# A decoder layer on one core: the recurrence's links cut into three steps, attention's calls between them in a fixed order, first query projections traced ahead of the inverse table

## The chip, the core and the metric

The kernel runs on one core of one Trainium2 chip. The metric is the device time of an execution in microseconds. TensorE (PE, with its weight loads PEld) multiplies, VectorE (DVE), ScalarE (ACT) and GpSimd (POOL) compute on the results, and SyncE (SP) issues the DMAs of this kernel, in order.

## The reference, cut to what matters

A layer takes x of 512 tokens by 1024 and adds three things to it in turn: half of a SwiGLU network, a mixing part, and half of a second SwiGLU network. The mixing part is the one that the change touches:

```python
proj = h @ w_in[l]
q, k, v, rr, rk, rv, rc = jnp.split(proj, split_idx, axis=-1)
...
att = dilated_attention(qh, kh, vh).transpose(0, 2, 1, 3).reshape(b, s, ATT_WIDTH)
rw = rwkv7_time_mix(rr, rk, rv, rc, ...)
x = x + jnp.concatenate([att, rw], axis=-1) @ w_out[l]
```

Attention has 8 heads of 64 and merges three dilated windows. The recurrence has 8 heads of 64, each with a 64x64 state that every token decays, corrects and adds to:

```python
sa = jnp.einsum('bhij,bhj->bhi', state, a_t)
state = state * w_t[:, :, None, :] + sa[..., None] * b_t[:, :, None, :] + v_t[..., None] * k_t[:, :, None, :]
return state, jnp.einsum('bhij,bhj->bhi', state, r_t)
```

## The kernel before

**Stages.** The first network runs to about 380 us, the mixing part to about 770 us (its output projection the last of it), the second network to the end. Matrices are kept as a high and a low fp32r half, and a product is three matmuls of 512 columns (`mm3`, L72), so one 128-column tile of a projection is 24 matmuls. The halves of a weight tile are made by ScalarE (L68) and by VectorE (L69) or POOL, from a load that SP issues (L64); there are two buffers of each half.

**The recurrence in chunks.** Its 512 tokens are cut into 8 chunks of 64. Inside a chunk the recurrence becomes triangular matrices, whose inverses `invert` (L632) makes on VectorE for all chunks and heads at once, 31 steps of two instructions; it ends with two transposes, ud and td, and with eight copies that make tm and um (L654, L655). `whole` (L661), called for each of four channel tiles, forms the off-diagonal blocks of the inverse table tbd: four products w, copies, four products u, copies.

**The chain.** `chain` (L855) is one link: for a pair of channel tiles and one chunk it multiplies the state into the chunk (cx, L866), multiplies that with the table (cs, L877) and forms the next state and the output (cn, L883). VectorE or ScalarE copies lie between the three. There are 16 links, (gi, c) with gi and c from 0 to 3; gi is a pair of tiles and a half of the sequence, and links of one pair depend on each other. `pre` (L805) loads and prepares a group of four links, `post` (L891) normalizes and gates its output. Both are generators in two parts.

**Attention.** `qkv` (L685) projects queries, keys and values of a channel tile (two heads) and is a generator that stops in the middle of each projection and between them. `attention` (L790) is a pipe of three: each call issues `scores` of a new unit (tile, block of 128 queries, head), `turned` (transposes) of the unit two calls back, and `weighted` of the unit three calls back. For the second head of a pair `weighted` ends with the transposition oT (L772) of what VectorE's rd and o (L768, L770) have made.

**What sets the order.** The framework's scheduler orders each engine's instructions at build time by readiness in its own model, and among ready ones by the order in which they were traced. `tc.high_priority()` puts what is traced in it ahead of older work. `tc.keep_in_program_order(t)` binds an instruction behind the one traced before it on its engine. Each engine then executes its instructions strictly in that order. The trace order of links, attention, projections, `pre` and `post` comes from a list of events with due times, sorted by time and then by a rank:

```python
ev += [(4 * gi + c, 4, lambda gi=gi, c=c: link(gi, c)) for gi in range(4) for c in range(4)]
ev += [(4 * gi + t, 5, lambda gi=gi: next(posts[gi], 0)) for t, gi in
       [(3, gi) for gi in range(4)] + list(zip((3.9, 3.9, 4.8, 4.5), range(4)))]
ev += [(4 * gi + c + t, 6, lambda u=(gi, c, h): attention(u)) for gi, t in enumerate((1.6, 1.0, 0.0, 0.0))
       for c in range(4) for h in range(2)]
for e in sorted(ev, key=lambda e: e[:2]):
    e[2]()
```

**Stores and ticks.** Operands of the chain pass through HBM tensors (ard, bkd, bvd). `put_stores` (L403), called in every projection of the recurrence, issues up to four stores that were collected before the last call, in program order on SP. `tick` (L396) runs work that was put off by so many half projections, as the bonus product (`bonus`, L623).

## Time and profile before

| | |
|---|---|
| Median of 3 runs | 1137.75 us (1137.55 to 1143.27) |
| Profiled execution | 1137.26 us, its span 1135.5 us |
| PE busy | 1100.3 us, 97% of the span, 5512 matmuls |
| DVE, ACT, POOL busy | 492.4, 383.9, 142.2 us |
| PE's granted clock, mean | 0.991 |

The page gives busy time by engine, the span in 40 slices, the chain of work that ended last and the costliest groups of instructions. A busy matmul is counted with its way through the array, so matmuls that follow each other every 0.23 us are shown as 0.39 us long and overlap. A number in square brackets behind an instruction is the idle time of its engine before it, with what ended it.

### The profile page before, as it was taken

Reading aid. Unit: us, or ns where it says so; the run is one execution under the profiler, and the core shown is the slowest. Engines: PE = TensorE matmul, PEld = TensorE weight load, DVE = VectorE, ACT = ScalarE, POOL = GpSimd, SP = SyncE. Lnnn points to the kernel's source line nnn. Section 1 sums busy time; section 2 is a strip of 40 time slices with the busy share of each in tenths; the row PEclk is TensorE's granted clock in tenths of the full one; section 3 lists DMA queues with packets and bytes.
Section 4 is the critical chain, followed back from the end, with each engine's and each line's share of the span. In section 5 each row is a group of like instructions: output and inputs, shape, how many; then the busy total and the mean of one; then the engine's idle time right before and its main releaser. Section 6 shows DMA issues by size and latency. Waiting matters only on the chain.

```text
span 1135.5 us, 13760 instructions
## 1 busy us (share of the span) xinstructions
PE 1100.3 (97%) x5512; PEld 918.6 (81%) x5512; DVE 492.4 (43%) x811; ACT 383.9 (34%) x604; POOL 142.2 (13%) x189
## 2 busy tenths in 40 slices
PE   7999999999999999898899999999999999999998
PEld 6888888888888977676788888789888888888887
DVE  5333333332223545594467568644333333332222
ACT  4332223222222356524344544433322232222120
POOL 3000000000000346303342221112000000000000
PEclk9999999999999999998989999999999999999999
DMA  5322322233224424442422201422223322233321
GB/s 189 111 93 94 104 99 93 93 98 103 96 93 146 164 70 102 121 123 82 130 57 66 84 29 29 141 83 94 93 93 103 101 93 93 96 103 101 126 94 56
DMA packets 53202, 111.88 MB, mean 99 GB/s; under 512 B 20721, under 2 KB 26097, under 8 KB 53138
## 3 DMA queue, kind: packets, MB, share of 16 engines
q1 hardware_dynamic: 53138, 111.00, 30.6%
q8 instruction: 43, 0.70, 0.3%
q14 instruction: 21, 0.17, 0.0%
HBM read 100.50 MB, written 9.44 MB: 97 GB/s over the span
## 4 chain that ended last, share of the span: by engine, by line
PE 48%; DVE 2%; POOL 2%; ACT 1%; issue 1%; POOLq 0%; ACTq 0%
PE gu L76 7%; PE gu L77 7%; PE gu L73 7%; PE accd L76 4%; PE accd L73 4%; PE accd L77 4%; PE in L77 1%; PE in L73 1%; PE in L76 1%; PE aa L840 1%; PE acco L76 1%; PE cn L883 1%; PE acco L77 1%; PE acco L73 1%; PE cx L866 1%; PE po L764 1%
## 5 line engine op out<-in xcount | busy, mean ns | idle before, releaser
L68 ACT CAST hi_gu<-raw_gu 128x1024 fp32r<-128x1024 f32 x88 | 92.8, 1054 | 316.2 <-PE gu L76 303.6
L69 DVE TENSOR_TENSOR lo_gu<-raw_gu,hi_gu 128x1024 fp32r<-128x1024 f32 x84 | 102.9, 1225 | 158.3 <-ACT hi_gu L68 154.3
L76 PE MATMUL accd<-lo_d,hh 128*128 128x512 f32 x288 | 112.3, 390 | 0.0
L77 PE MATMUL accd<-hi_d,hl 128*128 128x512 f32 x288 | 112.1, 389 | 0.0
L73 PE MATMUL accd<-hi_d,hh 128*128 128x512 f32 x288 | 112.0, 390 | 0.0
L69 DVE TENSOR_TENSOR lo_d<-raw_d,hi_d 128x1024 fp32r<-128x1024 f32 x44 | 53.3, 1224 | 127.5 <-ACT hi_d L68 127.1
L68 ACT CAST hi_d<-raw_d 128x1024 fp32r<-128x1024 f32 x44 | 45.6, 1053 | 152.7 <-PE accd L77 133.0
L198 DVE TENSOR_TENSOR sg<-gu,sg 128x512 f32<-128x512 f32 x44 | 30.4, 692 | 143.5 <-PE gu L77 142.1
L76 PE MATMUL gu<-xa0l,hi_gu 128*128 128x512 f32 (+1 forms) x184 | 70.0, 380 | 0.3 <-DVE xa0l L130 0.3
L73 PE MATMUL gu<-xa0h,hi_gu 128*128 128x512 f32 (+1 forms) x184 | 70.2, 381 | 0.1
L73 PE MATMUL gu<-xc0h,hi_gu 128*128 128x512 f32 (+1 forms) x184 | 70.0, 380 | 0.0
L73 PE MATMUL gu<-xa1h,hi_gu 128*128 128x512 f32 (+1 forms) x184 | 70.0, 380 | 0.0
L73 PE MATMUL gu<-xc1h,hi_gu 128*128 128x512 f32 (+1 forms) x184 | 70.0, 380 | 0.0
L76 PE MATMUL gu<-xc0l,hi_gu 128*128 128x512 f32 (+1 forms) x184 | 69.9, 380 | 0.0
L77 PE MATMUL gu<-xa0h,lo_gu 128*128 128x512 f32 (+1 forms) x184 | 69.9, 380 | 0.0
L77 PE MATMUL gu<-xa1h,lo_gu 128*128 128x512 f32 (+1 forms) x184 | 69.9, 380 | 0.0
L76 PE MATMUL gu<-xa1l,hi_gu 128*128 128x512 f32 (+1 forms) x184 | 69.9, 380 | 0.0
L77 PE MATMUL gu<-xc0h,lo_gu 128*128 128x512 f32 (+1 forms) x184 | 69.9, 380 | 0.0
L76 PE MATMUL gu<-xc1l,hi_gu 128*128 128x512 f32 (+1 forms) x184 | 69.9, 380 | 0.0
L77 PE MATMUL gu<-xc1h,lo_gu 128*128 128x512 f32 (+1 forms) x184 | 69.9, 380 | 0.0
L76 PEld LDWEIGHTS accd<-lo_d,hh 128*128 128x128 f32 x288 | 54.1, 188 | 11.6 <-DVE lo_d L69 0.5
L77 PEld LDWEIGHTS accd<-hi_d,hl 128*128 128x128 f32 x288 | 54.1, 188 | 11.3
(349 smaller groups left out, 2250.2 us busy)
## 6 DMA issues: line engine op xcount, KB each, us to landing
raw_gu<-in_ffn_w_gu SPq DMA_DIRECT2D x88, 512.0 KB, 3.4
raw_d<-in_ffn_w_down SPq DMA_DIRECT2D x44, 512.0 KB, 3.4
raw_in<-in_w_in SPq DMA_DIRECT2D x28, 512.0 KB, 3.8
raw_o<-in_w_out SPq DMA_DIRECT2D x8, 512.0 KB, 3.4
x<-in_x SPq DMA_DIRECT2D x4, 512.0 KB, 6.4
xd<-x SPq DMA_DIRECT2D x4, 512.0 KB, 2.6
xr<-ard SPq DMA_DIRECT2D x8, 256.0 KB, 4.5
bk<-bkd SPq DMA_DIRECT2D x4, 512.0 KB, 4.3
```

The source lines that it names most:

```text
L68: A.copy(out=hi, in_=raw)
L69: (lo_eng or V).tensor_tensor(out=lo, in0=raw, in1=hi.bitcast(F32), op=ALU.subtract)
L73: first = T.matmul(ps, lh, rh, start=start, stop=False)
L76: T.matmul(ps, lh, rl, start=False, stop=False)
L77: T.matmul(ps, ll, rh, start=False, stop=stop)
L198: V.tensor_tensor(out=sg, in0=ps[1], in1=sg, op=ALU.mult)
L764: T.matmul(po[:, h, 0:65], pw[:, j * P:(j + 1) * P], va[:, j, h, 0:65], start=(j == 0), stop=(j == qi))
L840: T.matmul(ps[:, c], bk[:, j, c], xr[:, j, c, 2 * h:2 * h + 2], start=True, stop=True)
L866: T.matmul(px[:, j, h], xr[:, j, c, 2 * h:2 * h + 2].rearrange("p a b -> p (a b)"), sv[:, j, h, c, :], start=True, stop=True)
L883: T.matmul(pn[:, j, h], kr[:, j, c, 2 * h:2 * h + 2].rearrange("p a b -> p (a b)"), sv[:, j, h, c, :], start=True, stop=True)
```

## The change

`put_stores` keeps stores back for one more call (`recent`). In `invert` the four copies of tm move from POOL to VectorE. In `whole` the first product w of a tile is bound in program order. `qkv` stops once more, after the query projection. The query projections of tiles 0 and 1 are traced right after `invert`, each followed by a tick, and `whole` after them, without ticks of its own. `chain` becomes a generator in three steps, the first matmul of each bound in program order; it is no longer traced at high priority. The due times of attention, of the projections of tiles 2 and 3 and of `post` are set anew, so that each link's steps are due at 0, 0.3 and 0.6 of its slot and two attention calls at 0.1 and 0.4 from slot 1 on.

```diff
--- before.py
+++ after.py
@@ -398,13 +398,14 @@
         for f in due.pop(turn[0], ()):
             f()
 
-    stores, older = [], []
+    stores, recent, older = [], [], []
 
     def put_stores():
 
         for out_, in_ in older[:4]:
             tc.keep_in_program_order(Q.dma_start(out=out_, in_=in_))
-        older[:] = older[4:] + stores
+        older[:] = older[4:] + recent
+        recent[:] = stores
         stores.clear()
 
     def proj_parts(j, ct):
@@ -651,7 +652,7 @@
         um, tm = (tmp([P, NCT, 4, 32], n) for n in ("um", "tm"))
         for h in range(2):
             for e in range(2):
-                G.tensor_copy(out=tm[quad(h, e)], in_=tv[quad(h, 0), :, :, e])
+                V.tensor_copy(out=tm[quad(h, e)], in_=tv[quad(h, 0), :, :, e])
                 G.tensor_copy(out=um[quad(h, 1 - e)], in_=uv[quad(h, 1), :, :, e])
         return ud.rearrange("p (a b c) t -> p a b c t", a=NCT, b=2), um, tm
 
@@ -668,7 +669,9 @@
         G.memset(w, 0.0)
         ps = pt([P, 4, 32], f"w{ct}")
         for m in range(4):
-            T.matmul(ps[:, m, :], R[ct]['nof'][:, m, :], tm[:, ct, m, :], start=True, stop=True)
+            t = T.matmul(ps[:, m, :], R[ct]['nof'][:, m, :], tm[:, ct, m, :], start=True, stop=True)
+            if m == 0:
+                tc.keep_in_program_order(t)
         for h in range(2):
             for e in range(2):
                 q_ = quad(h, 1 - e)
@@ -686,6 +689,7 @@
         tq = lambda shape, name: gp.tile(shape, F32, tag="tq", bufs=2, name=name)
         at = lambda shape, n, t=F32R: gp.tile(shape, t, tag=f"at{n}", bufs=2, name=f"{n}{ct}")
         acc = yield from proj_parts(0, ct)
+        yield
         sq = tq([P, S], f"sqq{ct}")
         A.activation(out=sq, in_=acc, func=AF.Square)
 
@@ -862,9 +866,11 @@
         jh = [(j, h) for j in range(2) for h in range(2)]
 
         px = pc([P, 2, 2, CH], f"cx{nm}")
-        for j, h in jh:
-            T.matmul(px[:, j, h], xr[:, j, c, 2 * h:2 * h + 2].rearrange("p a b -> p (a b)"), sv[:, j, h, c, :],
-                     start=True, stop=True)
+        for n, (j, h) in enumerate(jh):
+            t = T.matmul(px[:, j, h], xr[:, j, c, 2 * h:2 * h + 2].rearrange("p a b -> p (a b)"), sv[:, j, h, c, :],
+                         start=True, stop=True)
+            if n == 0:
+                tc.keep_in_program_order(t)
         xc = spool.tile([P, 2, 2, CH], F32, tag="cx", bufs=2, name=f"xc{nm}")
         V.tensor_copy(out=xc, in_=px)
         if not last:
@@ -872,16 +878,22 @@
             for h in range(2):
                 V.tensor_tensor(out=sp[half(h)], in0=sv[half(h), :, h, c, :],
                                 in1=pend[cp][half(h), :, cg:cg + 1].broadcast_to([64, 2, CH]), op=ALU.mult)
+        yield
         pa = pc([P, 2, 2, CH], f"cs{nm}")
         for j in range(2):
-            T.matmul(pa[:, j], tbd[:, gi, j, c, :], xc[:, j], start=True, stop=True)
+            t = T.matmul(pa[:, j], tbd[:, gi, j, c, :], xc[:, j], start=True, stop=True)
+            if j == 0:
+                tc.keep_in_program_order(t)
         A.copy(out=sv[half(0), :, 0, c, :], in_=pa[half(0), :, 0])
         V.tensor_copy(out=sv[half(1), :, 1, c, :], in_=pa[half(1), :, 1])
 
+        yield
         pn = ps_y.tile([P, 2, 2, CH], F32, tag="y", name=f"cn{nm}")
-        for j, h in jh:
-            T.matmul(pn[:, j, h], kr[:, j, c, 2 * h:2 * h + 2].rearrange("p a b -> p (a b)"), sv[:, j, h, c, :],
-                     start=True, stop=True)
+        for n, (j, h) in enumerate(jh):
+            t = T.matmul(pn[:, j, h], kr[:, j, c, 2 * h:2 * h + 2].rearrange("p a b -> p (a b)"), sv[:, j, h, c, :],
+                         start=True, stop=True)
+            if n == 0:
+                tc.keep_in_program_order(t)
         if not last:
             for h in range(2):
                 V.tensor_tensor(out=nxt[half(h), :, h], in0=pn[half(h), :, h], in1=sp[half(h)], op=ALU.add)
@@ -937,11 +949,14 @@
     for ct in range(NCT):
         rates(ct)
     inv = invert()
+    parts = [qkv(ct) for ct in range(NCT)]
+    for ct in range(2):
+        next(parts[ct])
+        next(parts[ct])
+        tick()
     for ct in range(NCT):
         whole(ct, *inv)
-        while due:
-            tick()
-    for out_, in_ in older + stores:
+    for out_, in_ in older + recent + stores:
         Q.dma_start(out=out_, in_=in_)
     pstack.close()
     gp = mc.enter_context(tc.tile_pool(name="gp", bufs=1, reuse_waits="tile"))
@@ -966,22 +981,22 @@
         for z in held:
             hilo(mixT[z[0]], *z[1:])
 
-    def link(gi, c):
-        with nullcontext() if gi == 2 else tc.high_priority():
-            chain(gi, c)
-
-
-    parts = [qkv(ct) for ct in range(4)]
-    ev = [(t, 1, lambda ct=ct: next(parts[ct], 0)) for ct, t0, dt in ((0, -1.0, 0.05), (1, -0.5, 0.05), (2, 4.0, 0.6), (3, 7.8, 0.6))
-          for t in (t0 + dt * n for n in range(6))]
+    links = {(gi, c): chain(gi, c) for gi in range(4) for c in range(4)}
+
+
+    ev = [(t, 1, lambda ct=ct: next(parts[ct], 0)) for ct, ts in enumerate((
+          (-1.0, -0.95, -0.9, -0.85, -0.8), (-0.5, -0.45, -0.4, -0.35, -0.3),
+          (2.8, 3.8, 4.8, 5.8, 6.4, 6.8, 7.4), (7.8, 8.4, 8.8, 9.4, 9.8, 10.4, 10.8))) for t in ts]
     ev += [(11.0, 1, mix)]
     ev += [(t, 2 + n, lambda gi=gi: next(pres[gi], 0)) for gi, ts in enumerate(((-2, -2), (2, 2), (5, 6), (9, 9)))
            for n, t in enumerate(ts)]
-    ev += [(4 * gi + c, 4, lambda gi=gi, c=c: link(gi, c)) for gi in range(4) for c in range(4)]
+
+    ev += [(4 * gi + c + t, 4, lambda gi=gi, c=c: next(links[gi, c], 0)) for gi in range(4) for c in range(4)
+           for t in (0, 0.3, 0.6)]
     ev += [(4 * gi + t, 5, lambda gi=gi: next(posts[gi], 0)) for t, gi in
-           [(3, gi) for gi in range(4)] + list(zip((3.9, 3.9, 4.8, 4.5), range(4)))]
-    ev += [(4 * gi + c + t, 6, lambda u=(gi, c, h): attention(u)) for gi, t in enumerate((1.6, 1.0, 0.0, 0.0))
-           for c in range(4) for h in range(2)]
+           [(3.7, gi) for gi in range(4)] + list(zip((4.3, 4.3, 4.8, 4.5), range(4)))]
+    ev += [(t + 0.1 + 0.3 * h, 6, lambda u=(ct, qi, h): attention(u)) for ct, ts in enumerate(
+           ((1, 2, 3, 4), (5, 6, 7, 7.5), (8, 9, 10, 11), (12, 13, 14, 15))) for qi, t in enumerate(ts) for h in range(2)]
     for e in sorted(ev, key=lambda e: e[:2]):
         e[2]()
     step = begin(mixT)
```

## Rows read from the trace of the kernel before

**Rows 1.** busy us (instructions) of PE, PEld, DVE, ACT, POOL; PEclk, DMA, GB/s

```profile
476.00:521.00 45.00, 40.19 (x163) 31.05 (x161) 42.11 (x84) 12.58 (x19) 3.83 (x4) 0.96 0.39 118
521.00:548.00 27.00, 21.76 (x115) 18.21 (x116) 8.07 (x19) 10.49 (x29) 11.03 (x19) 0.87 0.28 88
526.00:532.00 6.00, 5.76 (x19) 4.95 (x20) 1.70 (x3) 1.02 (x3) 3.75 (x8) 0.56 0.13 29
548.00:584.00 36.00, 33.15 (x202) 29.02 (x200) 19.20 (x50) 13.24 (x26) 16.33 (x22) 0.91 0.34 95
584.00:714.00 130.00, 124.20 (x877) 111.44 (x877) 93.41 (x271) 62.89 (x131) 32.82 (x37) 1.00 0.17 52
```

**Rows 2.** timeline of TensorE: start us, us, instruction, idle before and its releaser

```profile
482.77 0.50 PE L77 MATMUL in<-xb0h,lo_in 128*128 128x512 f32 x1 [2.82 <-DVE lo_in L69]
484.02 0.63 PE L73 MATMUL in<-xb0h,hi_in 128*128 128x512 f32 x1
```

**Rows 3.** timeline of TensorE round the inverse table's first product

```profile
520.37 0.39 PE L73 MATMUL in<-xb1h,hi_in 128*128 128x512 f32 x1
520.60 0.39 PE L76 MATMUL in<-xb1l,hi_in 128*128 128x512 f32 x1
526.24 1.91 PE L671 MATMUL w<-tm,nof 128*128 128x32 f32 x8 [5.26 <-POOL tm L654]
```

**Rows 4.** timelines of VectorE, POOL and ScalarE, the same columns

```profile
518.63 2.14 DVE L648 STREAM_TRANSPOSE td<-tu 128x1024 f32<-128x1024 f32 x1
...
525.58 0.61 POOL L654 COPY tm<-td 32x512 f32<-32x512 f32 x1
...
511.10 0.68 ACT L519 ACTIVATE v<-in,dv 128x512 f32<-128x512 f32 x1
```

**Rows 5.** groups on VectorE, 521 to 715: busy us, mean ns | idle before

```profile
L869 DVE COPY xc<-cx 128x256 f32<-128x256 f32 x16 | 6.7, 421 | 6.1 <-PE cx L866 5.6
...
L675 DVE COPY w<-w 32x128 f32<-32x128 f32 x8 | 2.3, 283 | 2.6 <-ACT w L675 2.5
...
L628 DVE TENSOR_TENSOR bv<-bo,v 128x512 f32<-128x512 f32 x1 | 0.7, 692 | 0.4 <-PE bo L626 0.4
```

**Rows 6.** timelines of POOL and VectorE during the inversion

```profile
477.67 1.19 POOL L615 TENSOR_TENSOR rt<-r,pb 128x512 f32<-128x512 f32 x1 [10.45 <-DVE r L520]
...
477.75 1.18 DVE L641 TENSOR_TENSOR pr<-au,tu 128x60 f32<-128x60 f32 x1
478.97 0.23 DVE L643 TENSOR_TENSOR tu<-tu,pr 128x60 f32<-128x60 f32 x1
```

**Rows 7.** TensorE's waits, 521 to 556 and 556 to 584: us, times, longest

```profile
PE in L73 <- ACT kts L704: 1.7, 1, 1.7
...
PE spk L511 <- ACT rbk L507: 1.2, 1, 1.2
```

**Rows 8.** timeline of TensorE at a link late in the chain

```profile
699.88 0.71 PE L877 MATMUL cs<-xc,tbd 128*128 128x128 f32 x4 [0.52 <-DVE xc L869]
```

**Rows 9.** TensorE's waits, 584 to 715

```profile
PE cn L883 <- DVE sv L879: 1.2, 2, 0.6
PE cs L877 <- DVE xc L869: 1.0, 2, 0.5
```

**Rows 10.** timelines of VectorE and TensorE at two of attention's outputs

```profile
596.62 0.15 DVE L768 RECIPROCAL rd<-po 128x2 f32<-128x2 f32 x1
...
598.18 0.29 DVE L770 TENSOR_TENSOR o<-po,rd 128x128 f32<-128x128 f32 x1
...
728.06 0.48 PE L76 MATMUL acco<-lo_o,mx0h 128*128 128x512 f32 x1
...
729.00 0.33 PE L772 MATMUL oT<-ident,o 128*128 128x128 f32 x1
```

**Rows 11.** timeline of TensorE, first output product on the recurrence's last part

```profile
733.18 0.84 PE L73 MATMUL acco<-hi_o,mx1h 128*128 128x512 f32 x3
```

**Rows 12.** timeline of ScalarE at a weight load

```profile
500.19 1.05 ACT L68 CAST hi_in<-raw_in 128x1024 fp32r<-128x1024 f32 x1 [1.75 <-DMA raw_in<-in_w_in]
```

## The prediction

> **What bounds the kernel now.** I read the page's engine table first: TensorE is busy almost all of the span, so whatever moves the end must shorten TensorE's stream, its waits or its slow clock. The change touches the mixing stage alone, and the second view cuts that by stretches [rows 1]. The idle time of a stretch is its length less PE's busy time. From 476 to 521 us it is 4.8 us, but there VectorE is busy 42.1 of 45 us with the triangular inversion, and TensorE waits for weight halves that VectorE makes [rows 2]; the change lightens none of that. After it the idle is 5.2 us (521 to 548), 2.9 (548 to 584) and 5.8 (584 to 714). The granted clock adds to that: 0.56 over the 6 us from 526 means 5.3 us at half speed, so 2.6 us lost; 0.91 over the 36 us from 548 means 6.5, so 3.2 us lost. The ceiling of any gain is 13.9 of idle and 5.8 of clock, 19.7 us. Then I read who waits for whom inside each stretch, and single timelines.
>
> **Part A, the inverse table (521 to 548 us).** TensorE's last projection matmul starts at 520.60; then TensorE stands 5.26 us until the fourth copy of tm has left POOL [rows 3]. VectorE had finished td at 518.63 + 2.14 = 520.77; POOL made tm and um by turns and began its fourth tm at 525.58 [rows 4].
> The headline move, query projections ahead of the table, I cost at nothing. ScalarE reads the last values accumulator of the recurrence at 511.10 [rows 4], so the matmuls from there to 520.6, 0.23 us apart [rows 3], are attention's projections already: the scheduler had put some 41 of them there. The change fixes that place and swaps a key projection for the second query projection, of the same size. The pin on the first table product adds no wait, since it stood behind these in any case. Without such cover 9.5 us would lie bare, but the pin forbids just that.
> The copy is what pays. No row shows a VectorE copy of 32x512 from SBUF. The nearest are copies from PSUM, 0.283 us with 128 elements and 0.421 with 256 [rows 5]: 0.14 for 128 more, so 0.70 with 512. Four cost 1.1 us if size were free and 2.8 by the slope; I take the slope, since both rows bear it. tm is then complete at 523.6, at best at 521.9, and at worst, with the last bonus product (0.69) [rows 5] ahead on VectorE, at 524.3. TensorE is done with projections at 520.8 and with the last bonus product, which now comes first, near 521.3. It waits 2.3 us (0.6 to 3.0) in place of 5.26: 3.0 us gained (2.3 to 4.7). For the clock the neighbour is a wait of 2.82 us, after which matmuls took 0.63 us [rows 2], not the usual 0.39 [rows 3]. 2.3 is shorter, by how much it must be no row says, so I take half of the 2.6 us. If a weight half also gets ahead of tm, most of the gain goes; that is the lower bound. **A: 4.3 us, from 1 to 7.**
> Behind tm's copies on VectorE stands the weight half of the key projection that fills the pauses of the table's products; it comes 2.8 us later, while TensorE runs the first products.
> One observation speaks against the split. A POOL product from 477.67 to 478.86 reads SBUF, and a VectorE product that began in it took 1.18 us, the next of its size 0.23 [rows 6]: the two held each other up. The Trainium skill, "SBUF — State Buffer", section "Who interferes with whom", says that POOL and a VectorE copy in a two-port mode exclude one another for a whole instruction; no row of before shows a copy doing that. By that rule tm's first copy would wait for um's last. um can start at 518.8 and takes about 0.6 us four times, so it ends near 521.3: 0.5 us less gain, inside the bounds. The same skill, "VectorE: DVE Perf Modes", section "Mode 2×_2P", would have such a copy make two elements a cycle; an estimate from its 0.96 GHz is 0.27 us each, and A would be nearer 6. The sum here goes by rows, and by neither.
>
> **Part B, from the table to the first links (548 to 584 us).** Lost now: 2.9 us of idle, namely 1.7 at a projection whose accumulator ScalarE had not yet freed and 1.2 at a transposition waiting for ScalarE's spread [rows 7], and 3.2 us of clock. Here links 0 to 3 lie among projections of tiles 0 and 1. After the change the first link is traced behind all of these, so the stretch becomes dense 512-column matmuls. TensorE now draws some 45 projection matmuls, 10 us, into the table's 27; if A is shorter some 15 of them are left over, 3.5 us, and cover the 1.7. The spread's chain then runs beside a whole projection. Against that, link 0 has no attention between its steps: three waits, each as the 0.52 us of a bare link [rows 8], 1.6 us unless later work floats up. I take 4 of the 6.1. **B: +4, from -1.6 to +6.**
>
> **Part C, links with attention (584 to 714 us).** Of the idle 5.8 us, waits of link steps are 1.2 at cn and 1.0 at cs [rows 9]: 2.2 us is all that filling can return, as links and attention overlap already. An attention call's scores, transposes and weighted products last longer than the 0.52 us they have to cover.
> The added wait hides in the pin. The cs step is held behind the instruction traced before it on TensorE, and every other attention call ends with the transposition oT, which waits for VectorE's rd and o. In the last unit TensorE was free at 728.06 and oT ran at 729.00: 0.94 us [rows 10]. Behind it on TensorE would stand cs and cn, and behind those the next link. Fifteen links have it. Fillers are projection halves up to link 10, and later the next unit's scores and transposes, so I charge 0.1 us a link, 1.5 in all. **C: +0.7, from -12 (nothing fills: 14.1 less 2.2) to +2.2.** Dropping the links' high priority costs nothing as long as trace order puts them first anyway.
>
> **Part D, the tail.** The last link and the last post now follow both last attention calls. The first matmul on that post's result ran at 733.18 [rows 11], 19 us after the last link, and those 19 us have to be filled from what is left; some 3 us of it, the two calls, have gone ahead. Output matmuls that need attention alone can still come forward. **D: -1, from -3 to 0.**
>
> **Stores.** Each goes out one projection later on SP's in-order queue, where weight loads stand behind it. A late load reached an engine visibly once: ScalarE waited 1.75 us for it [rows 12], and TensorE did not. I take 0 (0 to 1.7). Stores that fall behind the table delay the reloads after it, which the dense projections of B cover; bare, a pair of loads costs its landing. Tiles 2 and 3's seven parts and the later posts shift work between links: nothing, while TensorE has other work.
>
> **Sum.** 4.3 + 4 + 0.7 - 1 = 8.0 us off the profiled execution's 1137.26 gives 1129.3. The median of the three runs lies 0.5 higher, 1129.8; I round to 1129.5.
>
> **Rivals.**
> *VectorE sets the table after all.* tm goes behind the bonus product and a weight half, table products start near 525.5, the clock still falls, and the slack that feeds B is missing: A 1, B 1, C and D as above, 1.7 us in all, about 1136. For: VectorE is 94% busy until 521. Against: tm is traced ahead of that half. The same time comes out if the change doesn't do what it says: a pin binds one instruction to the one before, and later work may float past it into the old order. I count both as one.
> *oT paces the links*, the slower one. Its price then includes VectorE's queue: at 596.62 + 0.15 rd was done, and o came at 598.18 [rows 10], 1.4 us after it could. 0.94 + 1.4 less 0.8 of filler is 1.5 a link, 23 us for fifteen. With A, B, D and the 2.2 gained (9.5 us) that is 1137.3 - 9.5 + 23 = 1151. It decides from 0.63 us a link on (no gain), and from 1.04 it is over 0.5% slower. For: o waited behind other VectorE work there. Against: the pin makes o urgent in the order, and projections are at hand for ten links.
> *All of it fits*: A 7, B 6, C 2.2, D 0, 15.2 us, 1122. For: each idle place has a named cause. Against: B needs both waits and the clock.
>
> **Chances.** Forecast 0.45, VectorE (or old order) 0.25, oT 0.18, all of it 0.12. About 0.5% is what a measurement of this kernel tells from no change; the bounds are 1132.1 and 1143.4. The forecast's own spread, A from 1 to 7 and B from -1.6 to 6, has a little on the wrong side, the rivals a little on the right: faster 0.57, same 0.25, slower 0.18. The range leaves out most of the oT case and the end of the best: 1119 to 1143.
>
> **What would show it.** A: the wait before the first w matmul between 0.6 and 3 us and named VectorE's tm; full clock from 526. B: granted clock 1.0 where links 0 to 3 begin, no wait at spk. C: waits at cs for oT or o would be the slower rival; cn and cs without waits, the forecast. D: more idle before 733's counterpart. I am wrong if idle plus lost clock from 521 to 714 does not fall below some 12 us, or if the stretch before 521, held unchanged, moves by over 2 us.

## The result and the profile after

The changed kernel takes 1150.62 us (median; 1148.69 to 1151.61) against 1137.65 for the kernel before: a ratio of 1.0108, 95% interval 1.0074 to 1.0142. It is 1.1% slower, 13.0 us, where 1129.5 had been forecast. The profiled execution took 1151.33 us with a span of 1149.5; its mean granted clock is 0.982, before 0.991. Runs of one kernel differ in their mean granted clock (the kernel before from 0.982 to 0.992), so medians below come with their lowest and highest run where that matters.

The first view gives the same stretches as [rows 1], and two more (the stretch and its length; busy us and instructions of PE, PEld, DVE, ACT, POOL; PEclk; DMA; GB/s):

```profile
476.00:521.00 45.00, 39.46 (x166) 30.59 (x164) 43.35 (x87) 13.41 (x23) 7.71 (x10) 1.00 0.39 117
521.00:548.00 27.00, 23.60 (x118) 19.77 (x119) 11.26 (x25) 13.11 (x32) 7.90 (x17) 0.82 0.34 101
548.00:584.00 36.00, 33.12 (x220) 28.97 (x219) 17.54 (x50) 14.37 (x27) 15.09 (x14) 0.95 0.32 93
584.00:714.00 130.00, 120.01 (x777) 106.67 (x775) 84.42 (x241) 52.48 (x109) 29.43 (x34) 0.93 0.16 49
598.00:621.00 23.00, 19.22 (x114) 17.77 (x113) 16.80 (x45) 8.71 (x19) 6.17 (x7) 0.78 0.12 35
705.00:719.00 14.00, 12.34 (x55) 11.49 (x55) 6.87 (x25) 5.51 (x14) 3.12 (x3) 0.52 0.01 2
```

From 521 to 714 us TensorE idles 3.4 + 2.9 + 10.0 = 16.3 us (13.9 before), and the clock takes 4.9 + 1.8 + 9.1 = 15.8 (before 3.5 + 3.2 = 6.7 if counted so; the prediction's 5.8 leaves out half clock while TensorE stood). The link stretch, at full clock before, has it now at 0.93; the last two rows are where. In the second of them the clock is at the lower of its two levels (1.2 of 2.4 GHz) nearly throughout.

Clock times of the two kernels are no longer comparable, so the second cut goes by events: from the last table product (547.3 before, 542.8 after) to the last projection product, and from there to the first transposition of the next network (757.2 and 771.3). First before, then after:

```profile
547.30:685.70 138.40, 132.05 (x885) 117.60 (x885) 89.81 (x249) 61.07 (x123) 43.76 (x52) 0.98 0.23 69
685.70:757.20 71.50, 67.30 (x404) 57.35 (x403) 47.49 (x114) 32.75 (x67) 12.63 (x16) 1.00 0.29 97
```

```profile
542.80:691.00 148.20, 136.19 (x881) 120.24 (x881) 88.64 (x248) 60.61 (x123) 42.66 (x52) 0.94 0.22 67
691.00:771.30 80.30, 72.59 (x403) 62.33 (x402) 48.26 (x116) 32.48 (x67) 12.15 (x16) 0.91 0.23 83
```

TensorE's instructions are the same in number, within four in each part. The changed kernel arrives 4.5 us earlier, then loses 9.8 us while projections last and 8.8 us after them: 14.1 in all (the spans differ by 14.0). By kind, TensorE's busy time over the whole span grows from 1100.3 to 1109.4 us with the same 5512 matmuls, and its idle time from 35.2 to 40.1: some 9 of the 14 us are products at half clock (the mean clock's fall by 0.009 gives 10), 5 are waiting. In the second part nothing but links, attention and posts is there until the output projection, which starts only behind the last link: 29.0 us without a projection before (685.7 to 714.7), 42.1 after (691.0 to 733.1).

Who TensorE waits for, 543 to 771 (us, times, longest), the counterpart of [rows 7, 9]:

```profile
PE yo L928 <- DVE ysb L923: 3.3, 2, 1.7
PE in L73 <- ACT kts L708: 2.8, 1, 2.8
PE sc L744 <- DVE mx L748: 2.1, 1, 2.1
PE spk L512 <- ACT rbk L508: 1.9, 1, 1.9
PE po L768 <- DVE pw L759: 1.6, 2, 1.4
PE oT L776 <- DVE o L774: 1.4, 3, 0.7
...
PE cs L884 <- DVE xc L875: 0.8, 2, 0.5
```

Of these names yo and gg are transposes and gate products of `post`, aa products of `pre`, kts and spk belong to the keys of `qkv`, and sc, po and oT to attention. The link steps themselves hardly wait: cs 0.8 in all, cx and cn not at all. The waits stand in what lies ahead of them. Two stretches of TensorE's timeline show it (start, duration, instruction, idle before and its releaser). From link 4 to link 5:

```profile
598.95 0.56 PE L768 MATMUL po<-va,pw 128*128 128x65 f32 x4
601.59 0.51 PE L744 MATMUL sc<-kh,qs 128*128 128x512 f32 x1 [2.08 <-DVE mx L748]
...
607.58 0.78 PE L893 MATMUL cn<-sv,kr 128*128 128x64 f32 x6
...
610.75 1.05 PE L496 MATMUL hsq<-cst,sqq 128*128 128x2 f32 x8 [1.04 <-ACT o L934]
...
617.04 3.52 PE L844 MATMUL aa<-xr,bk 128*128 128x128 f32 x16
620.32 0.47 PE L73 MATMUL in<-xb0h,hi_in 128*128 128x512 f32 x1
620.63 1.05 PE L844 MATMUL aa<-xr,bk 128*128 128x128 f32 x8
621.52 1.00 PE L870 MATMUL cx<-sv,xr 128*128 128x64 f32 x8
```

Link 4 is done at 608.36 and link 5's own input is there at 609.06 (VectorE's sv, 608.46 + 0.60), but link 5 begins at 621.52, pinned behind all 32 aa products of the next group. Between 596.3 and 620.3 no projection begins. From link 12 to link 13:

```profile
704.94 1.34 PE L893 MATMUL cn<-sv,kr 128*128 128x64 f32 x8
...
710.83 1.12 PE L928 MATMUL yo<-ident,ysb 128*128 128x128 f32 x4 [1.66 <-DVE ysb L923]
711.74 1.92 PE L940 MATMUL gg<-sg,g 96*128 96x256 f32 x4
713.45 1.81 PE L870 MATMUL cx<-sv,xr 128*128 128x64 f32 x8
```

Link 13 needs nothing from yo and gg, products of the third post, but is pinned behind them; its own input was there at 706.94 (VectorE's sv, 706.33 + 0.61).

### The profile page after: what moved, and what is told of

Same layout as the page of the kernel before. It is cut to its first block, busy times and chain, and to the rows that moved or that the text cites. A ratio compares the mean times of both kernels' runs of the same rounds, so it can differ in the third digit from the quotient of the medians.

```text
span 1149.5 us, 13743 instructions
## 1 busy us (share of the span) xinstructions
PE 1109.4 (97%) x5512; PEld 926.6 (81%) x5512; DVE 494.1 (43%) x815; ACT 383.9 (33%) x604; POOL 138.1 (12%) x185
## 4 chain that ended last, share of the span: by engine, by line
PE 84%; DVE 7%; POOL 3%; ACT 3%; issue 2%; DMA 1%; SPq 0%; POOLq 0%; ACTq 0%; DVEq 0%
PE gu L73 14%; PE gu L76 14%; PE gu L77 14%; PE accd L76 7%; PE accd L73 7%; PE accd L77 7%; PE in L73 3%; PE in L77 3%; PE in L76 2%; PE aa L844 1%; PE cn L893 1%; DVE pr L642 1%; PE acco L77 1%; PE acco L73 1%; PE acco L76 1%
## 5 line engine op out<-in xcount | busy, mean ns | idle before, releaser
L73 PEld LDWEIGHTS accd<-hi_d,hh 128*128 128x128 f32 x288 | 53.9, 188 | 11.5 <-ACT hi_d L68 0.4
```

The lines of the kernel that those rows point to most:

```text
L73: first = T.matmul(ps, lh, rh, start=start, stop=False)
```

## The experiments

Ratios are to the kernel before, with 95% intervals.

### Which half loses?

The first half alone: before with the change's edits to `put_stores`, `invert` and `whole` and its early query projections; links, events and priority stay.

```diff
+        if ct < 2:
+            yield
...
-          for t in (t0 + dt * n for n in range(6))]
+          for t in (t0 + dt * n for n in range(5 if ct < 2 else 6))]
```

> Before with the change's first half alone: tm's copies on VectorE, stores kept back for one more call, the query projections of tiles 0 and 1 traced ahead of the table's products, the pin on the first w. Links, events and priority as before. Theory: the loss of the change sits in the links, and this half is the gain that the trace of after shows at the last u (542.78 us against 547.33, 4.55 us ahead); the links then run as before, so about 1133 us (1130 to 1135). Rival: this half is what upsets the later stages, because projections of tiles 0 and 1 that used to lie among the first links are gone; then 1140 or more.

Measured: 1142.71 us (1130.13 to 1145.08), ratio 1.002 (0.9988 to 1.0051). Its fastest run has a mean clock of 0.995, its slowest 0.979. The profiled one shows where (the granted clock is the third column from the end):

```profile
696.00:718.00 22.00, 20.71 (x94) 19.68 (x95) 11.59 (x39) 7.79 (x19) 3.10 (x3) 0.53 0.01 1
```

So neither expectation holds as it stands. The rival's time came (1140 or more), though not among the first links alone: the gain is there in some runs, and in the profiled one most of it is lost to half clock behind the last projection.

The links' half alone: after with those edits undone.

```diff
-          (-1.0, -0.95, -0.9, -0.85, -0.8), (-0.5, -0.45, -0.4, -0.35, -0.3),
+          (-1.0, -0.95, -0.9, -0.85, -0.8, -0.78, -0.75), (-0.5, -0.45, -0.4, -0.35, -0.3, -0.28, -0.25),
```

> After with the first half taken back: tm on POOL, stores as before, no early query projections, no pin on w; chain in three pinned steps, no high priority and the new due times stay. Theory: this half loses all that after loses behind the last u, 18.7 us (228.5 us from there to the first output tile of the next network against 209.9), so about 1155 us (1151 to 1158). Rival (the first half is to blame): 1137, as before.

Measured: 1155.26 us, 1.0169 (1.0142 to 1.0196). The theory's time came: the links' half loses 17.6 us, and the first half gives back 4.6 of them.

### Does oT pace the links?

```diff
-        ps = pt([P, P], f"oT{ct}{qi}")
-        T.transpose(out=ps, ...)
+        AT['late'] = lambda: outputs(ct, qi, o)   # run behind the next call's scores
```

> After with attention's transposition oT and what follows it issued in the next attention call behind that call's scores, so that no link step stands directly behind an oT that waits for VectorE; pins, due times and the rest stay. The recorded slower rival (oT paces the links, 1.5 us a link): 10 us or more come back, 1140 or less. The theory of pins behind preparations and posts: waits that name oT and its inputs are 1.4 to 2 us in all in after, so 1148 to 1151.

Measured: 1146.90 us, 1.0092 (1.0073 to 1.0110): 3.7 us back, not 10, and more than the other theory's 1148 to 1151 allowed. The recorded slower rival had the right time for the change, 1151, but its mechanism is worth a quarter of what it charged.

### The pins

Without the pins on cx, cs and cn (the edit for cx is shown, the others are like it):

```diff
             t = T.matmul(px[:, j, h], ...)
-            if n == 0:
-                tc.keep_in_program_order(t)
```

> After without the program-order pins on cx, cs and cn; due times, three steps, priority and the first half stay. Theory: the pins lose the time, since they hold each link behind group preparations, posts and ScalarE's and VectorE's work for these, and then TensorE's clock falls in the sparse stretches; without them most of 18.7 us comes back: about 1135 us (1131 to 1140). Rival A, the new due times and the lost high priority do it: 1147 to 1151. The recorded slower rival (oT in front of cs) also expects about 1135 here.

Measured: 1145.62 us, 1.0071 (1.0046 to 1.0095): 5.0 us back, a third of what was expected. The rest stays with what is left of the links' half: the due times, the three steps and the lost high priority, which no run separates.

The edit above alone, the pins on cs and cn kept:

> After without the pin on each link's first step cx alone; the pins on cs and cn stay. Theory: what the pins cost (5.0 us, 1150.6 against 1145.6 without any) is that cx waits behind group preparations and posts, as link 0 behind spk, link 5 behind the aa products and link 13 behind yo and gg: 1146 to 1148. Rival: cs and cn behind attention's and VectorE's work cost it: 1150 to 1151.

Measured: 1143.98 us (1143.08 to 1148.37), 1.0068 (1.0041 to 1.0096). 6.6 us come back, so the pin on cx carries all of the pins' cost; those on cs and cn cost nothing that can be told.

### The hole in the projections

In the changed kernel no half of tile 2's projections is due between 3.8 and 5.8: the hole. The changed kernel with these due times at about those of before:

```diff
-          (2.8, 3.8, 4.8, 5.8, 6.4, 6.8, 7.4),
+          (4.0, 4.6, 4.65, 5.2, 5.8, 6.4, 7.0),
```

> After with the parts of tile 2's projections due at about the times of before (4.0, 4.6, 4.65, 5.2, 5.8, 6.4, 7.0 in place of 2.8, 3.8, 4.8, 5.8, 6.4, 6.8, 7.4); pins stay. In after no projection half is due between 3.8 and 5.8, and from about 598 to 620 us TensorE has only small matmuls; the clock is half from 603.2 to 606.6 and 613.4 to 620.2. Theory of the hole: with projections there the half clock of that stretch goes, 10.2 us at half speed or 5.1 us, so about 1145 us (1142 to 1147). Rival: waits of the pinned links make the clock fall, wherever the projections are: 1149 to 1152.

Measured: 1145.12 us, 1.0071 (1.0043 to 1.0099), as the hole's theory gave. The stretch that had 0.78 above, with the pins still there:

```profile
598.00:621.00 23.00, 22.23 (x155) 19.32 (x154) 16.14 (x44) 10.39 (x23) 7.04 (x7) 1.00 0.11 35
698.00:712.00 14.00, 12.34 (x55) 11.50 (x54) 6.36 (x23) 5.07 (x11) 3.13 (x3) 0.51 0.00 1
```

The half clock at the end of the links is untouched (second row). The reverse, the hole put into the kernel before:

```diff
+          for t in ((2.8, 3.8, 5.8, 6.4, 6.8, 7.4) if ct == 2 else ...)]
```

> Before with one thing changed: tile 2's projection halves due at 2.8, 3.8, 5.8, 6.4, 6.8 and 7.4 as in after, in place of 4.0 to 7.0 in steps of 0.6. No pins, one-piece links, first half as before. Theory of the hole: half clock appears near 600 to 622 us, 10 to 17 us of it, so 5 to 8 us more: about 1143 (1141 to 1146). Rival: without pins the stretch stays at full clock: 1136 to 1139.

Measured: 1145.89 us (1136.68 to 1148.15), 1.0050 (1.0022 to 1.0078), slower without one pin:

```profile
616.00:624.00 8.00, 6.86 (x35) 6.67 (x36) 4.92 (x13) 2.34 (x6) 1.18 (x2) 0.57 0.33 95
701.00:723.00 22.00, 20.47 (x92) 19.21 (x92) 12.28 (x43) 6.61 (x18) 3.10 (x3) 0.53 0.00 1
```

The first row is the expected place, but it holds 3.4 us of lost clock where 5 to 8 were expected. The larger loss, 10.3 us, is the second row, which was not expected: links that come later leave the last projection (688.8) farther from the first output product (724.9, 36.1 us against 29.0).

Nor does a hole bring half clock every time. Without the pin on cx (the run above), tile 2's due times are still those of the change, and 20.1 us pass without a projection at full clock:

```profile
594.30:614.40 20.10, 16.96 (x130) 15.05 (x128) 16.46 (x44) 10.09 (x21) 6.18 (x7) 1.00 0.12 40
```

Without any pin the clock is half from 605.4 to 622.5 in a hole of 26.3 us (596.6 to 622.9). What decides between the two is not shown; there is one trace of each kernel. In these traces the repair of cx and the repair of the hole take the same half clock away, so the 6.6 and the 5.5 are in good part one saving.

Both repairs, no pins and tile 2's old times:

> After without the three pins and with tile 2's parts due as before: both repairs. Without pins alone 1145.6, with half clock from 605.4 to 622.5 us. Theory of the hole: that episode goes, 17 us at half speed or 5 to 8 us: about 1138.5 (1136 to 1141). Rival: something else in the new order (posts, attention) makes it fall: 1144 to 1147.

Measured: 1141.91 us (1138.29 to 1145.10), 1.0033 (1.0011 to 1.0056). This lies between the two expectations. The clock from 598 to 621 is full; half clock now comes at 657 and 711. Not all of the sum arrives.

### The stores

The kernel before with `recent` alone:

```diff
-        older[:] = older[4:] + stores
+        older[:] = older[4:] + recent
+        recent[:] = stores
```

> Before with one thing changed: stores kept back for one more projection. Theory: this alone takes away the 2.82 us wait for a weight half at 482.77 and the half clock behind it, since the weight load goes out on SP at 461.4, ahead of a store, and not at 466.6 behind two, so that VectorE splits the weight before the inversion begins; the last table product u, at 547.33 in before, ends at 543.5 to 545.5 (tm is still on POOL), and the time is 1133 to 1136 unless the clock falls more often later. Rival: the gain before 521 us belongs to the query projections or to tm on VectorE: u at 547, 1137 to 1138.

Measured: 1139.56 us, 1.0014 (0.9998 to 1.0031): no gain, and above both expectations. The mechanism is there, SP's load of that weight goes out ahead of a store, as in the changed kernel, here before and after:

```profile
461.63 2.24 SPq L406 DMA_DIRECT2D ard<-at  x2
...
466.55 0.60 SPq L64 DMA_DIRECT2D raw_in<-in_w_in  x1
```

```profile
461.43 0.34 SPq L64 DMA_DIRECT2D raw_in<-in_w_in  x1
461.88 1.56 SPq L406 DMA_DIRECT2D ard<-at  x2
```

VectorE then splits the weight ahead of the inversion, and the wait of 2.82 us [rows 2] and its half clock are gone in both. But with the stores alone TensorE has used up the projections when the table comes, and stands there instead:

```profile
524.60 1.92 PE L672 MATMUL w<-tm,nof 128*128 128x32 f32 x8 [4.12 <-POOL tm L655]
543.49 1.89 PE L679 MATMUL u<-um,w 128*128 128x32 f32 x8 [2.64 <-DVE w L676]
548.53 1.89 PE L679 MATMUL u<-um,w 128*128 128x32 f32 x8 [1.45 <-DVE w L676]
```

Its last u is over at 550.2, later than before (547.3).

And after with that edit undone:

> After with the stores going out as before, all else kept. Theory: the wait for a weight half near 482 us is back, and the last u, at 542.78 in after, ends 4 us later, at 546 to 548; the time is 1152 to 1156. Rival: the gain before 521 us comes from the early query projections or from tm on VectorE: u at 543, 1149 to 1152.

Measured: 1150.66 us, 1.0118 (1.0091 to 1.0145), the same as with the new stores. The wait is back (2.85 us at 482.13, first w at 524.38 and not 521.42), but the last u begins at 542.52, 0.6 us later than in after, not 4. So here the rival's figures came, and the theory that the stores gain time failed twice: what they gain ahead of the table is taken back at it.

### Added work in the bare stretches

Three 512-column products, overwritten at once, into each of eight pT tiles, first in the changed kernel with tile 2's old times:

```diff
         pT = pm([P, S], f"pT{ct}{qi}{h}")
+        if (2, 3) <= (ct, qi) <= (3, 2):
+            z = QKV[3][0][0]
+            for _ in range(3):
+                T.matmul(pT, z[:, 0, 0:P], z[:, 0, :], start=True, stop=True)
```

> After with tile 2's parts due as before (1145.1 without more) and with added work: three 512-column products, whose result is overwritten, into each pT tile of eight attention calls from block 3 of tile 2 on, 24 in all, 5.5 us at 0.23 us each. Theory that the clock falls where TensorE has small products without projections for long: the half clock of 698.2 to 711.9 goes (6.8 us back) and the added work costs at most 5.5, less what falls into waits: 1140 to 1144, with the granted clock full from 690 to 730. Rival: waits alone set the clock, or the added work only costs: 1147 to 1151.

Measured: 1143.66 us (1141.03 to 1146.85), 1.0040 (1.0014 to 1.0066). This is within the theory's range. With 5.5 us more work it is no slower than without (1145.12), and of the half clock from 698 to 712 a quarter is left:

```profile
698.00:712.00 14.00, 11.42 (x70) 10.09 (x69) 8.56 (x27) 6.61 (x15) 3.14 (x3) 0.88 0.00 1
```

The same edit in the first half alone:

> The first half alone (1142.7, from 1130.1 to 1145.1) with the same 24 added products. Theory: the half clock from 696.8 to 717.3 in the run profiled goes, and with it the spread between runs; 1130 plus at most 5.5: 1133 to 1137 in every run, faster than before in spite of 5.5 us more work. Rival: the added work only costs: 1145 or more.

Measured: 1138.45 us (1132.17 to 1145.52), 1.0005 (0.9979 to 1.0030). This is above the 1133 to 1137 expected of every run. The half clock from 696 to 718 is gone, the rest of the spread (520, 544, 565) is not.

Nothing added, tile 3's last halves later:

```diff
+          for t in ((7.8, 8.4, 9.0, 10.0, 11.0, 11.9) if ct == 3 else ...)]
```

> The first half alone with the last three projection halves of tile 3 due at 10.0, 11.0 and 11.9 in place of 9.6, 10.2 and 10.8, so that projections lie among links 11 to 13 and nothing is added. Theory: the stretch without projections gets shorter by some 10 us, the half clock from 696.8 on is shorter or gone: 1131 to 1138. Rival: the later values hold up attention's last tile, and waits there cost as much: 1141 to 1146.

Measured: 1142.01 us (1133.05 to 1145.41), 1.0019 (0.9992 to 1.0046): a miss. The half clock from 696 to 717 is there all the same, although the stretch from the last projection to the first output product is 25.6 us (687.57 to 713.15) and not 36.4 as without it, shorter even than the 29.0 of the kernel before. The length of that stretch alone does not decide whether the clock falls.

Then added work in all four places of the first half's kernel, 43 products: `dense(ps, 12)` ahead of the first w, 10 ahead of the first vt, 5 ahead of the first spk, two in each pT.

```diff
+    def dense(ps, n):
+        z = xT[0][0]
+        for _ in range(n):
+            tc.keep_in_program_order(T.matmul(ps, z[:, 0, 0:P], z[:, 0, :], start=True, stop=True))
```

> The first half alone with added 512-column products, overwritten before use, where its clock fell: 12 ahead of the first table product w (TensorE stands 4.0 us there), 10 ahead of the first vt (3.1 us of waiting for kts behind it), 5 ahead of the first spk (1 us), and two, not three, in each of the eight pT tiles; 43 in all, 9.9 us at 0.23 us each, some 7 of them inside waits. Theory: only the clock takes the first half's gain; with full clock from 520 to 730 the time is that of its fastest run, 1130.1, plus 2 to 3: 1131 to 1135 in nearly all runs, faster than before. Rival: the added work costs what the clock gives: 1137 to 1141.

Measured: 1131.03 us (1129.02 to 1132.07), 0.9935 (0.9915 to 0.9956). With 9.9 us more work the first half is 11.7 us faster than without it, and 0.65% faster than the kernel before: as the theory had it, and the fastest of all kernels here.

### What each half is worth with the added products

The same 43 products in the kernel before, in after with tile 2's old times, and in that without pins.

> Before with the same 43 added products (12 ahead of the table's products, 10 ahead of the first vt, 5 ahead of the first spk, two in each of eight pT tiles), 9.9 us of work. Theory: the first half's gain is its own and comes to 4 to 5 us when the clock stays full, so that this kernel stands above the first half with the same products (1131.0): 1134 to 1137. Rival: only the clock counted, and the added products alone make before as fast: 1130 to 1132.

Measured: 1140.32 us, 1.0021 (1.0005 to 1.0038). This is above both expectations: the added work does not help the kernel before. The first half, with the same added work, is worth 1140.3 - 1131.0 = 9.3 us (some 3 of it clock: 0.991 against 0.994). The same products lie in different waits in the two kernels, so part of the 9.3 may be what they cost the kernel before.

> After with tile 2's parts due as before and the same 43 added products; pins stay. With the clock near full in both, the difference to the first half with these products (1131.0) is what the new links cost by their order alone. Theory: 6 to 9 us, from waits behind pinned steps: 1137 to 1140. Rival: the new links cost by the clock alone: 1130 to 1134.

Measured: 1143.87 us (1143.53 to 1144.26), 1.0060 (1.0043 to 1.0078). The new links cost 12.8 us over the first half alone, more than either theory said, and not by their order alone: the clock did not hold (0.991 against 0.994).

> The same as the run before without the three pins. If the pins make what the links lose at full clock: 1131 to 1134. If the new due times make it (the first link stands behind both tiles' projections, attention's last calls among the last links): the same time as with pins, 1137 to 1140.

Measured: 1136.62 us (1133.86 to 1141.00), 0.9993 (0.9974 to 1.0013), between the two expectations. 7.2 us are the pins', and 5.6 are left to the due times, the three steps and the priority. The three kernels, each from its last table product to its last projection product and from there to the next network; first half, changed links with pins, without pins:

```profile
538.30:679.60 141.30, 136.85 (x907) 121.12 (x907) 90.47 (x249) 60.47 (x123) 43.11 (x52) 0.98 0.23 71
679.60:750.80 71.20, 69.41 (x419) 60.04 (x418) 47.48 (x114) 32.99 (x67) 12.05 (x16) 1.00 0.29 97
```

```profile
538.50:680.90 142.40, 136.49 (x906) 119.28 (x906) 89.14 (x248) 60.82 (x123) 44.53 (x52) 0.99 0.24 72
680.90:764.30 83.40, 76.30 (x420) 65.26 (x419) 48.40 (x116) 32.54 (x67) 11.74 (x16) 0.92 0.24 80
```

```profile
539.70:679.60 139.90, 135.34 (x907) 120.20 (x907) 90.32 (x248) 61.43 (x123) 44.66 (x52) 0.99 0.24 73
679.60:755.00 75.40, 70.12 (x419) 59.78 (x418) 47.80 (x116) 32.87 (x67) 10.98 (x16) 1.00 0.25 88
```

While projections last, the three are within 2.5 us. The cost of the new links lies behind the last projection: 12.2 us with pins, 4.2 without. Of the 12.2, 5.3 are idle time (7.1 against 1.8) and the rest is the clock, 0.92; without pins the clock is full in that stretch, 35.8 us of which have no projection. With pins TensorE waits 2.5 us at yo for VectorE's ysb, which waits for POOL, and link 13's cx stands behind it:

```profile
699.68 0.69 DVE L939 TENSOR_TENSOR ysb<-ysb,gw 128x512 f32<-128x512 f32 x1 [1.53 <-POOL gw L938]
```

All three repairs at once, without the added work at the table:

> After with three repairs: no pin on cx (6.6 us alone), tile 2's parts due as before (5.5 alone), three 512-column products in each of eight pT tiles at the end of the links (6.8 of half clock back for at most 5.5 of work). Theory that these causes add up: 1150.6 - 6.6 - 5.5 - 1.5 = 1137 (1135 to 1140). Rival: they overlap, since each acts through the same clock, and one hides the next: 1141 to 1144.

Measured: 1147.05 us (1143.78 to 1151.17), 1.0080 (1.0048 to 1.0111): a miss. The profiled run, at 1143.78, has a clock of 0.992, so here the 24 added products (5.5 us) and idle time stand against the savings: 2.9 us at kts, 2.5 at yo, 1.9 at spk. The other three runs are at 1144.0, 1150.1 and 1151.2. Savings of single repairs (6.6 for cx, 5.5 for the hole) came largely through the same clock and do not add. Why the median is not even at the 1143.7 of the kernel that keeps the pin on cx stays open.

## Why the prediction was wrong, point by point

**The account.** After less before is 13.0 us. Of it 5.5 are the hole in tile 2's projections (1150.6 to 1145.1). With the same added work in both, and the hole closed, the change still loses 1143.9 - 1140.3 = 3.6: the first half gains 9.3, the new links take 12.8. The remaining 4 us are by difference, the clock at those waits that the added work held up, against what that work cost; that part was not measured by itself. Without added work the same sum reads 17.6 lost by the links' half (near 12.8 + 5.5) and 4.6 given back by the first half, about half of its 9.3.

**The stretch before 521, held unchanged within 2 us: wrong.** The first w came 4.8 us earlier (521.42 against 526.24, [rows 3]). Without the new stores it came 1.9 earlier, so 3.0 are the stores'. The step that failed for this stretch is "I take 0 (0 to 1.7)" for the stores: it asked only what the delayed stores hold up, not what the loads gain by going ahead of them. For the time of the whole kernel the 0 held (1150.66 with the old stores, 1150.62 with the new).

**A: size right, partly by luck, its signs wrong.** The wait ahead of w is 3.96 us, not 2.3. It is named VectorE's tm, as said, but the clock fell all the same:

```profile
517.07 0.40 PE L76 MATMUL in<-xb0l,hi_in 128*128 128x512 f32 x1
521.42 1.89 PE L672 MATMUL w<-tm,nof 128*128 128x32 f32 x8 [3.96 <-DVE tm L655]
```

TensorE had run out of projections at 517, since the stores let it run ahead; with the old stores the wait is 2.98 us, within the 0.6 to 3.0 forecast, and the clock falls behind it too (0.50 from 524 to 530). The last u ended 4.5 us earlier, beside the 4.3 forecast.

VectorE's copies were priced by the slope at 0.70 us each, and four took 2.70, 0.675 each. But that mean hides two prices (least, median and longest ns of one in the last four rows; the very last is the kernel before):

```profile
518.58 2.70 DVE L655 COPY tm<-td 32x512 f32<-32x512 f32 x4
...
516.85 2.65 POOL L656 COPY um<-ud 32x512 f32<-32x512 f32 x4 [13.88 <-DVE ud L648]
```

```profile
L655 DVE COPY tm<-td x4: 454/731/739, 518.6 to 520.5; 32x512 f32<-32x512 f32 x4
L656 POOL COPY um<-ud x4: 604/608/708, 516.9 to 518.8; 32x512 f32<-32x512 f32 x4
L669 POOL MEMSET w<- x4: 520/742/802, 519.6 to 521.7; 128x512 f32 x4
L668 POOL MEMSET w<- x4: 523/524/526, 526.9 to 528.3; 128x512 f32 x4
```

VectorE's first copy took 0.45 us, the other three 0.73 to 0.74. Beside them POOL was slower too: its last copy of um took 0.71 us against 0.60, and its memsets of w up to 0.80 against the 0.52 of the kernel before, where VectorE makes no tm. So the two engines held each other up, mainly over the memsets, and the slope, taken from copies out of PSUM, met the mean by luck: what was measured is a shorter copy and a wait. By these rows the hold-up cost tm some 0.8 us (an estimate: three times 0.73 less 0.45); no run moved the memsets.

The mutual hold-up that the Trainium skill gives ("SBUF — State Buffer", section "Who interferes with whom") thus shows in this trace, though not as the prediction worked it out, with tm's first copy behind um's last. Nor do the rows speak against the two elements a cycle of the Trainium skill, "VectorE: DVE Perf Modes", section "Mode 2×_2P": at one element a cycle of that page's 0.96 GHz a copy would take 0.53 us (an estimate), and the first took 0.45.

**B: +4 forecast, not there in the plain kernel.** The wait for kts grew from 1.7 to 2.8 us with half clock behind it, spk from 1.2 to 1.9. The leftover products that should have covered it were gone. Only with added work in those waits do A and B come to 9.3 us, against 8.3 forecast, and that as a difference of two kernels that both carry it.

**C: +0.7 forecast, -12.8 found, plus 5.5 for the hole.** The oT charge, 0.1 us a link, 1.5 in all, was about right as a wait: TensorE waits 1.4 us for attention's o, 2.6 at oT in all (moving oT gave 3.7 us back). The step that failed is the one before it: it looked for what a pinned step stands behind, and named only oT at cs. cx stands behind whatever was traced last, and that is aa, gg or spk of groups whose data depend on VectorE, ScalarE and POOL. The lower bound of -12 comes near the links' loss, but was put on another place. The second failed step is "Tiles 2 and 3's seven parts ... nothing, while TensorE has other work": tile 2 has no half due from 3.8 to 5.8, and there was no other dense work. The prices of the two steps overlap: in the trace without the pin on cx the hole is there and its half clock is not.

**D: -1 forecast, +5.1 measured.** From the last link to the next network 43.4 us before (713.74 to 757.18), 38.3 after (733.02 to 771.31): the attention calls had gone ahead of the links, and were paid for there.

**The tests.** Idle plus lost clock from 521 to 714, to be below some 12 us, is 32.1 (20.6 before, counted the same way). But "cn and cs without waits, the forecast" came true but for 0.8 us at cs, while the forecast did not: the waits sat one instruction further ahead, where no test looked.

**The rivals.** "oT paces the links" gave 1151, met within half a microsecond by chance; its mechanism is worth 3.7 us. The clock was counted in the prediction only as a thing to gain, 5.8 us; no rival had it fall where it was full.

## What to carry to other kernels

A pin on an in-order engine makes a step wait for everything traced ahead of it, so list those instructions, with what each waits for, and not only the one that seems to matter. Dense work is a stock: drawing it forward to fill one gap opens another where it used to lie, so look for long stretches without it after the change. They are where the clock can fall, not where it must: 20.1 and 35.8 us without a projection ran at full clock in two traces here, and most of 25.6 us at half in a third. Count the clock as something that can be lost as well; where a saving comes through it, savings of separate edits do not add.

## What the runs showed of the hardware

The same kernel came out between 1130.1 and 1145.1 us on one chip, with mean granted clocks from 0.995 to 0.979: in stretches of links and attention with waits of half a microsecond to two between small products, the clock was sometimes full, sometimes half. And 43 products that nobody uses, 9.9 us of TensorE's work, made that kernel 11.7 us faster. VectorE's copies of 32x512 between tiles in SBUF and POOL's copies and memsets of the same time held each other up: 0.45 us against 0.73 for the copy, 0.52 against 0.80 for the memset.
